# A transformer block on one Trainium2 core: the mixer's output gate copied out of PSUM by VectorE instead of ScalarE, and the three kinds of weight tile in one ring of twelve buffers

## The chip, the cores and the metric

The kernel runs on one of the eight cores of one Trainium2 chip. A time is the device time of one execution in microseconds (us), and a kernel's time is the median of its runs. The names of the engines are those of the profile: PE (TensorE, matrix multiplication; PEld is its weight load), DVE (VectorE), ACT (ScalarE), POOL (GpSimd) and SP (SyncE, which here does nothing but issue DMA transfers).

## The reference

One residual block over 512 tokens of width 1024, all in fp32. In short:

```python
mod = silu(c) @ w_ada + b_ada                        # nine rows of 1024: shift, scale, gate for three parts
sh1, s1, g1, sh2, s2, g2, sh3, s3, g3 = split(mod, 9)
x = x + 0.5 * g1 * swiglu(rms(x) * (1 + s1) + sh1, ffn1_w_in, ffn1_w_out)    # 2816 hidden features
x = x + g2 * mixer(rms(x) * (1 + s2) + sh2)
x = x + 0.5 * g3 * swiglu(rms(x) * (1 + s3) + sh3, ffn2_w_in, ffn2_w_out)

def mixer(h):
    gq, gk, gv, gz, ga, gb, cq, ckv, kr = split(h @ w_in)
    o_a = gated_delta_rule(silu(conv(gq, gk, gv)), ga, gb)       # 4 heads, chunks of 64
    o_a = rms(o_a) * silu(gz)                                    # gz is the output gate: z in the kernel
    o_b = block_causal_attention(cq, ckv, kr)                    # 4 heads, low-rank q and kv, rotary key
    return concat(o_a, rms(o_b)) @ w_out
```

## The kernel before, in words

Activations lie transposed, features on the 128 partitions and the 512 tokens along the free dimension. A product with a weight matrix goes by units of 128 output features. A unit's weights come as a raw fp32 tile of 128x8x128, which is 4 KB per partition and 512 KB in all, and are split into a high part and a low part. `wr` names the raw tile (`load`, L118, a DMA issued on SP's queue), `wh` the high part (`split_w`, L193, a cast on ACT) and `wl` the low part, raw minus high (L198, a subtraction on DVE). A few units, marked `dma`, form the low part otherwise: ACT writes minus raw, or rather its rounded copy (L195), and a DMA issued by POOL adds the raw tile onto it (L196). These are five units of the mixer's `w_in` and the first four of `ffn2_w_in`. PE then runs three matmuls for each of the eight slices of 128 inputs: high times high (L266), high weight times low activation (L267) and low weight times high activation (L268), 24 matmuls of 128x512 for a unit. The accumulator is one of the three PSUM buffers of pool `psa` (names `pa`). Five others (`psb`, names `pb`) serve all the rest.

The tiles `wr`, `wh` and `wl` come out of the pool `wp` (L85). It gives each tag its own ring of buffers, four each, twelve in all, 48 KB per partition. A raw tile is free again as soon as its split has read it, and a high or low tile only once PE has finished with the unit.

The order of the instructions in each engine's queue isn't written out by hand. A scheduler takes the instructions by the priorities that the program sets (`in_order`, `behind`), by the data that they need and by the buffers that the pools have free in its own reckoning of time, and writes one fixed queue for each engine. An engine works its queue strictly from front to back, and an instruction waits at the front until what it needs has come. So a pool of another shape moves instructions also in places that don't use it.

The program runs these stages, and the times are those of the profile. To 66 us: setup and `phase0`, which holds the first three pairs of units of the first feed-forward. 66 to 270 us: the rest of the first feed-forward's input (`ffn1`, L618, pairs of units 3 to 21), with `ada_rest` as side work. For that, SP loads the modulation weights into tiles `ar` (512 KB, pool `early`, three buffers), DVE multiplies and adds each into a sum `aa` (L549, then L551; six buffers), and PE adds up the columns of four sums at a time (L570), which frees them. 270 to 390 us: its output product (`down`). 390 to 720 us: the mixer. The last four units of `w_in` give the output gate z; `z_done` (L1919) copies each accumulator out of PSUM (L1921), and `gated_out` (L1681) reads z much later. Around them PE has the attention's scores (L1847, L1850), transposes of probabilities (L1867), and the blocks of the triangular inverse (L1553 to L1598). On ACT stand the exponentials `pr` (L168) with their ACT_TABLE_LOAD, and `mh` (L1905), on DVE the row maxima `mx` (L1856) and `ml` (L1906). 720 to 1076 us: the second feed-forward.

Of the kernel before, what the change touches and what calls it, by code (L numbers as in the profile page):

```python
# [11 lines left out]
F32 = mybir.dt.float32  # L12
F32R = mybir.dt.float32r
# [5 lines left out]
P = 128  # L19
# [22 lines left out]
class Side:  # L42


    def __init__(self, wide=1):
        self.todo, self.open, self.wide, self.at = [], [], wide, 0

    def add(self, *gens):
        self.todo.extend(gens)
# [30 lines left out]
class Block:  # L80
    def __init__(self, ctx, tc, ins, out):
        self.ctx, self.tc, self.nc, self.ins, self.out = ctx, tc, tc.nc, ins, out
        self.cp = ctx.enter_context(tc.tile_pool(name="cp", bufs=1))
        self.sp = ctx.enter_context(tc.tile_pool(name="sp", bufs=4))
        self.wp = ctx.enter_context(tc.tile_pool(name="wp", bufs=4))  # L85
        self.slots = ctx.enter_context(tc.tile_pool(name="slots", bufs=56))
        self.late = None
        self.psa = ctx.enter_context(tc.tile_pool(name="psa", bufs=3, space=bass.MemoryType.PSUM))
        self.psb = ctx.enter_context(tc.tile_pool(name="psb", bufs=5, space=bass.MemoryType.PSUM))
        self.n = 0  # L90
        self.mod = {}
        self.specs, self.ready = [], []
        self.tabled = None
# [104 lines left out]
        self.nc.vector.tensor_tensor(out=lo, in0=raw, in1=hi.bitcast(F32), op=ALU.subtract)  # L198

    def w_tiles(self):  # L200
        t = lambda dt, tag: self.wp.tile([P, 8, P], dt, tag=tag, name=self.name(tag))
        return t(F32, "wr"), t(F32R, "wh"), t(F32R, "wl")

    def unit(self, src, kts=8, dma=False):
# [536 lines left out]
    def pair_tasks(self, f, base, add):  # L741


        nc, v, w = self.nc, self.nc.vector, self.ins["ffn2_w_in"][0]
        r = {}
        flat = lambda t: t.rearrange("p k f -> p (k f)")
        A, B = slice(0, NT), slice(NT, 2 * NT)

        def tiles(names, tags, dt, bufs):
            for n, tag in zip(names, tags):  # L750
                r[n] = self.ws.tile([P, 2 * NT], dt, tag=tag, name=self.name(tag), bufs=bufs)

        def load():
            for n, c in (("g", f * P), ("u", DFF + f * P)):
                t = self.wp.tile([P, 8, P], F32, tag="wr", name=self.name("wr"))
                self.load(t, w[:, c:c + P].rearrange("(k p) f -> p k f", p=P))
                r[n] = flat(t)

        def sums():
            tiles(("x", "y"), ("sx", "sy"), F32, 1)  # L760
            v.tensor_tensor(out=r["y"][:, A], in0=r["g"][:, A], in1=r["g"][:, B], op=ALU.add)  # L761
            v.tensor_tensor(out=r["x"][:, A], in0=r["u"][:, A], in1=r["g"][:, A], op=ALU.add)

        def sums2():
            v.scalar_tensor_tensor(out=r["x"][:, B], in0=r["y"][:, A], scalar=-1.0, in1=r["u"][:, A], op0=ALU.mult,
                                   op1=ALU.subtract)
            v.tensor_tensor(out=r["y"][:, B], in0=r["u"][:, B], in1=r["x"][:, B], op=ALU.subtract)

        def hi(name, src, part=slice(0, 2 * NT)):
            def go():  # L770
                if name == "g1":
                    r["g1h"], r["g1l"] = self.slot(F32R, "gh"), self.slot(F32R, "gl")
                elif name == "y":
                    tiles(("yh", "yl"), ("yh", "yl"), F32R, 2)
                else:
                    for e in "hl":
                        r[name + e] = flat(self.wp.tile([P, 8, P], F32R, tag="w" + e, name=self.name("w" + e)))
                nc.scalar.copy(r[name + "h"], r[src][:, part])
            return go

        def lo(name, src, part=slice(0, 2 * NT)):
            def go():
                v.tensor_tensor(out=r[name + "l"], in0=r[src][:, part], in1=r[name + "h"].bitcast(F32), op=ALU.subtract)  # L783
            return go

        def early_copy(name, part):
            def go():
                if name not in r:
                    r[name] = self.slot(s=name)
                nc.scalar.copy(r[name][:, part], r["A"][:, :HALF])  # L790
            return go

        L, H = slice(0, HALF), slice(HALF, NT)

        def both():
            v.tensor_tensor(out=r["cc"], in0=r["cc"], in1=r["BC"], op=ALU.add)

        def gate0():
            v.tensor_tensor(out=r["uc"][:, H], in0=r["uc"][:, L], in1=r["BC"][:, H], op=ALU.add)
            nc.scalar.activation(r["uc"][:, H], r["uc"][:, H], AF.Silu, scale=-1.0)  # L800

        def gate1():
            nc.scalar.activation(r["cc"][:, H], r["cc"][:, H], AF.Silu, scale=-1.0)

        def act1():
            v.tensor_tensor(out=r["cc"][:, H], in0=r["cc"][:, H], in1=r["A"][:, :HALF], op=ALU.mult)

        def act0():
            v.tensor_tensor(out=r["cc"][:, L], in0=r["cc"][:, L], in1=r["uc"][:, H], op=ALU.mult)
            r["ah"] = self.slot(F32R, "ah")  # L810
            nc.scalar.copy(r["ah"], r["cc"])  # L811

        def act_low():
            al = self.slot(F32R, "al")
            v.tensor_tensor(out=al, in0=r["cc"], in1=r["ah"].bitcast(F32), op=ALU.subtract)
            self.act.append((r["ah"], al))

        r["do"] = dict(load=load, sums=sums, sums2=sums2)
        for n, src, part in (("u", "u", slice(0, 2 * NT)), ("x", "x", slice(0, 2 * NT)), ("y", "y", slice(0, 2 * NT)), ("g1", "g", B)):
            r["do"][n] = hi(n, src, part), lo(n, src, part)  # L820
        for i, (at, go) in enumerate(((-11, load), (-7, sums), (-5, sums2), (-6, hi("u", "u")), (-4, lo("u", "u")), (-4, hi("x", "x")),
                       (-3, lo("x", "x")), (-3, hi("y", "y")), (-2, lo("y", "y")), (-1, hi("g1", "g", B)),
                       (0, lo("g1", "g", B)), (1, early_copy("cc", L)), (4, early_copy("uc", L)), (7, early_copy("cc", H)),
                       (8, both), (9, gate1), (11, act1), (13, gate0), (15, act0), (16, act_low))):
            by_hand = 11 if base == 0 else 1 if base == 7 else 0
            if i >= by_hand:
                add(base + at, go)
        return r
# [21 lines left out]
    def ffn2_rest(self, ps):  # L850

        nc = self.nc
# [66 lines left out]
        w1 = self.ins["ffn2_w_in"][0]  # L919

        def raw(i):
            t = self.wp.tile([P, 8, P], F32, tag="wr", name=self.name("wr"))
            c = (i % 2) * DFF + (i // 2) * P
            self.load(t, w1[:, c:c + P].rearrange("(k p) f -> p k f", p=P))
            return t
# [1 line left out]
        raws, split, accs = {}, {3: self.next_unit(ahead=0)}, {0: ps[0], 1: ps[1], 2: ps[2]}  # L927

        def unit_split(i):
            hi, lo = (self.wp.tile([P, 8, P], F32R, tag=t, name=self.name(t)) for t in ("wh", "wl"))  # L930
            nc.scalar.copy(hi, raws[i])
            split[i] = hi, lo
            yield
            nc.vector.tensor_tensor(out=lo, in0=raws[i], in1=hi.bitcast(F32), op=ALU.subtract)
# [26 lines left out]
        for i in (4, 5, 6, 7):  # L961
            raws[i] = raw(i)
        steps = [T(0), T(1), T(2), unit_split(4), glu(0), (products, 3), T(3), unit_split(5), (do["load"],), (products, 4), T(4),
                 glu(1), unit_split(6), T(5), (products, 5), of(do["sums"]), of(do["sums2"]), unit_split(7), (d0[0],), T(6),
                 of(do["u"]), glu(2), (products, 6), of(do["x"]), (do1["load"],), T(7), of(do["y"]), of(tuple(d0[1:])),
                 (products, 7), glu(3), of(do["g1"])]
# [11 lines left out]
        k0, m = 16, 6  # L978
        units, ends = {}, {}

        def unit_load(t):
            raw = self.wp.tile([P, 8, P], F32, tag="wr", name=self.name("wr"))[:, :m, :]
            self.load(raw, w2[k0 * P:(k0 + m) * P, t * P:(t + 1) * P].rearrange("(k p) f -> p k f", p=P))
            units[t] = [raw]

        def unit_hi(t):
            units[t] += [self.wp.tile([P, 8, P], F32R, tag=w, name=self.name(w))[:, :m, :] for w in ("wh", "wl")]
            nc.scalar.copy(units[t][1], units[t][0])

        def unit_lo(t):  # L990
# [25 lines left out]
        for t in range(4, KT):  # L1016
            unit_load(t)
# [23 lines left out]
        t = KT - 1  # L1041
# [867 lines left out]
    def mixer(self, nb):  # L1909
        nc, tc = self.nc, self.tc  # L1910
# [7 lines left out]

        def z_done(i, p):  # L1919
            z = self.slot(s="z")  # L1920
            nc.scalar.copy(z, p)  # L1921
            self.zT.append(z)

        def conv_done(ct0, dst):
# [181 lines left out]
```

## Time and profile before

| | before |
|---|---|
| runs | 1077.47, 1080.53 and 1081.85 us, median 1080.53 us |
| the profiled execution | 1077.71 us, of which the span from the first to the last instruction is 1076.0 us |
| granted clock of PE, mean over the span | 0.987 |
| PE busy | 1046.7 us (97% of the span) |
| DVE, ACT, POOL busy | 689.4, 445.3 and 51.3 us |
| moved by DMA | 136.85 MB, mean 127 GB/s |

So 1.7 us of the profiled execution lie outside the span, and it was 2.8 us quicker than the median of the runs. In the lines of the profile, L12 is line 12 of the kernel, `out<-in` names tiles without their numbers, and a bracket such as [4.29 <-ACT z L1921] says that the engine had been idle 4.29 us, most of it until that instruction was done. A row of a timeline begins with start and duration in us. A row of windows gives a stretch, its length, the busy time of PE, PEld, DVE, ACT and POOL with their counts, then the clock granted to PE, the busy share of the DMA engines and the GB/s that they moved.

### The profile page before, as it was taken

Reading aid. Unit: us, or ns where it says so; the run is one execution under the profiler, and the core shown is the slowest. Engines: PE = TensorE matmul, PEld = TensorE weight load, DVE = VectorE, ACT = ScalarE, POOL = GpSimd, SP = SyncE. Lnnn points to the kernel's source line nnn. Section 1 sums busy time; section 2 is a strip of 40 time slices with the busy share of each in tenths; the row PEclk is TensorE's granted clock in tenths of the full one; section 3 lists DMA queues with packets and bytes.
Section 4 is the critical chain, followed back from the end, with each engine's and each line's share of the span. In section 5 each row is a group of like instructions: output and inputs, shape, how many; then the busy total and the mean of one; then the engine's idle time right before and its main releaser. Section 6 shows DMA issues by size and latency. Waiting matters only on the chain. (4 is left out here: it accounts for less than half of the span.)

```text
span 1076.0 us, 15659 instructions
## 1 busy us (share of the span) xinstructions
PE 1046.7 (97%) x6183; PEld 899.1 (84%) x6183; DVE 689.4 (64%) x1231; ACT 445.3 (41%) x761; POOL 51.3 (5%) x103
## 2 busy tenths in 40 slices
PE   6999999999999999998999899999999999999998
PEld 5788878788887898887778578988899999999997
DVE  4488983433577445558868644769768787777633
ACT  3342222222222245566575363465534444444322
POOL 1000000000000011102000030220000000000000
PEclk8999999999999999999999898999999999999999
DMA  9989963233698349411203001153432333233222
GB/s 274 277 240 310 301 203 99 81 98 93 199 289 263 95 120 240 113 49 40 79 25 92 26 21 39 40 126 91 129 107 79 118 115 98 83 118 99 67 71 79
DMA packets 203687, 136.85 MB, mean 127 GB/s; under 512 B 13777, under 2 KB 186590, under 8 KB 203614
## 3 DMA queue, kind: packets, MB, share of 16 engines
q1 hardware_dynamic: 202318, 131.14, 41.1%
q0 software_dynamic: 1296, 4.72, 2.4%
q8 instruction: 48, 0.79, 0.3%
q14 instruction: 25, 0.20, 0.1%
HBM read 128.63 MB, written 2.49 MB: 122 GB/s over the span
## 5 line engine op out<-in xcount | busy, mean ns | idle before, releaser
L266 PE MATMUL pa<-hh,wh 128*128 128x512 f32 (+1 forms) x597 | 227.0, 380 | 4.3 <-ACT z L1921 4.3
L268 PE MATMUL pa<-hh,wl 128*128 128x512 f32 (+1 forms) x597 | 225.0, 377 | 2.7 <-DMA wl<-wr 2.7
L267 PE MATMUL pa<-hl,wh 128*128 128x512 f32 (+1 forms) x597 | 224.8, 377 | 0.0
L193 ACT CAST wh<-wr 128x1024 fp32r<-128x1024 f32 (+1 forms) x106 | 108.0, 1019 | 258.3 <-PE pa L267 184.4
L198 DVE TENSOR_TENSOR wl<-wr,wh 128x1024 fp32r<-128x1024 f32 (+1 forms) x97 | 114.4, 1180 | 99.0 <-ACT wh L193 94.5
L266 PE MATMUL pa<-ah,wh 128*128 128x512 f32 (+1 forms) x396 | 145.5, 367 | 0.6 <-DVE xT L873 0.4
L267 PE MATMUL pa<-al,wh 128*128 128x512 f32 (+1 forms) x396 | 144.5, 365 | 0.0
L268 PE MATMUL pa<-ah,wl 128*128 128x512 f32 (+1 forms) x396 | 143.5, 362 | 0.0
L266 PEld LDWEIGHTS pa<-hh,wh 128*128 128x128 f32 x597 | 113.6, 190 | 27.2 <-ACT z L1921 4.7
L268 PEld LDWEIGHTS pa<-hh,wl 128*128 128x128 f32 x597 | 113.5, 190 | 23.1 <-DMA wl<-wr 3.3
L267 PEld LDWEIGHTS pa<-hl,wh 128*128 128x128 f32 x597 | 113.5, 190 | 19.2 <-DVE hl L453 0.4
L268 PEld LDWEIGHTS pa<-ah,wl 128*128 128x128 f32 x396 | 74.8, 189 | 12.0
L266 PEld LDWEIGHTS pa<-ah,wh 128*128 128x128 f32 x396 | 75.2, 190 | 10.4 <-ACT wh L193 1.7
L267 PEld LDWEIGHTS pa<-al,wh 128*128 128x128 f32 x396 | 75.2, 190 | 7.2
L551 DVE SCALAR_TENSOR_TENSOR aa<-ar,sc,aa 128x512 f32<-128x512 f32 x98 | 73.2, 751 | 9.7 <-DMA ar<-in_w_ada 8.5
L846 PE MATMUL pb<-fh,wh 128*128 128x256 f32 x144 | 40.7, 282 | 0.0
L848 PE MATMUL pb<-fh,wl 128*128 128x256 f32 x144 | 40.7, 283 | 0.0
L848 PE MATMUL pb<-hh,wl 128*128 128x256 f32 x144 | 40.7, 283 | 0.0
L847 PE MATMUL pb<-fl,wh 128*128 128x256 f32 x144 | 40.7, 282 | 0.0
L847 PE MATMUL pb<-hl,wh 128*128 128x256 f32 x144 | 40.7, 282 | 0.0
L846 PE MATMUL pb<-hh,wh 128*128 128x256 f32 x144 | 40.6, 282 | 0.0
L873 DVE SCALAR_TENSOR_TENSOR xT<-pa,mod,xT 128x512 f32<-128x512 f32 (+1 forms) x40 | 29.4, 736 | 17.5 <-PE pa L268 17.5
(433 smaller groups left out, 1995.0 us busy)
## 6 DMA issues: line engine op xcount, KB each, us to landing
wr<-in_ffn_w_in SPq DMA_DIRECT2D x82, 512.0 KB, 4.1
ar<-in_w_ada SPq DMA_DIRECT2D x48, 512.0 KB, 5.9
wr<-in_ffn_w_out SPq DMA_DIRECT2D x34, 512.0 KB, 3.4
ar<-in_w_ada SPq DMA_DIRECT2D x48, 256.0 KB, 4.8
wr<-in_w_in SPq DMA_DIRECT2D x21, 512.0 KB, 3.9
wr<-in_ffn_w_out SPq DMA_DIRECT2D x17, 384.0 KB, 3.4
wl<-wr POOLq DMA_DIRECT2D x9, 512.0 KB, 5.6
wr<-in_w_out SPq DMA_DIRECT2D x8, 512.0 KB, 4.8
```

Source lines behind the costliest of these rows:

```text
L193: self.nc.scalar.copy(hi, raw)
L198: self.nc.vector.tensor_tensor(out=lo, in0=raw, in1=hi.bitcast(F32), op=ALU.subtract)
L266: mm(out, wh, xh, start=start, stop=False)
L267: mm(out, wh, xl, start=False, stop=False)
L268: mm(out, wl, xh, start=False, stop=stop)
L551: nc.vector.scalar_tensor_tensor(out=acc, in0=a, scalar=sc, in1=acc, op0=ALU.mult, op1=ALU.add)
L846: mm(out, wh, xh, start=start and k == 0, stop=False, **kw)
L847: mm(out, wh, xl, start=False, stop=False, **kw)
L848: mm(out, wl, xh, start=False, stop=stop and k == 3, **kw)
L873: nc.vector.scalar_tensor_tensor(out=self.xT[t][:, ts], in0=p[:, ts], scalar=gate[:, t:t + 1], in1=self.xT[t][:, ts], op0=ALU.mult, op1=AL ...
```

## The change

It has two parts. The pool `wp` gets twelve buffers, and every tile of it takes the one tag "w", so raw, high and low tiles share one ring of the same twelve buffers. And z is copied out of PSUM by DVE.

```diff
@@ class Block, __init__
-        self.wp = ctx.enter_context(tc.tile_pool(name="wp", bufs=4))
+        self.wp = ctx.enter_context(tc.tile_pool(name="wp", bufs=12))
@@ w_tiles
-        t = lambda dt, tag: self.wp.tile([P, 8, P], dt, tag=tag, name=self.name(tag))
+        t = lambda dt, tag: self.wp.tile([P, 8, P], dt, tag="w", name=self.name(tag))
         return t(F32, "wr"), t(F32R, "wh"), t(F32R, "wl")
...
@@ the same at L755, L777, L922, L930, L982 and L987, for instance
-                t = self.wp.tile([P, 8, P], F32, tag="wr", name=self.name("wr"))
+                t = self.wp.tile([P, 8, P], F32, tag="w", name=self.name("wr"))
...
@@ mixer, z_done
             z = self.slot(s="z")
-            nc.scalar.copy(z, p)
+            nc.vector.tensor_copy(z, p)
             self.zT.append(z)
```

Each engine still has the instructions that it had, but for z, and the queues stand in another order. Three places follow, each with the queue of before and then that of the change. The numbers tell tiles of one name apart.

First, SP's queue in the first feed-forward. This is the stretch of before that runs from the load ar_802 on; `ar` are modulation weights, `wr` raw weights of feed-forward units, whose order of use is wr_627, 633, 669, 731, 766, 820, 855, 942, 977, 1034, 1070.

```order
L118 DMA ar_802<-in_w_ada 128x2x512
L118 DMA ar_851<-in_w_ada 128x2x512
L118 DMA ar_886<-in_w_ada 128x2x512
L118 DMA wr_977<-in_ffn_w_in 128x8x128
L118 DMA ar_891<-in_w_ada 128x2x512
L118 DMA ar_973<-in_w_ada 128x2x512
L118 DMA ar_1008<-in_w_ada 128x2x512
L118 DMA wr_1034<-in_ffn_w_in 128x8x128
L118 DMA ar_1012<-in_w_ada 128x2x512
L118 DMA wr_1070<-in_ffn_w_in 128x8x128
```

And this is the stretch of the changed queue with the same modulation loads.

```order
L118 DMA wr_731<-in_ffn_w_in 128x8x128
L118 DMA ar_851<-in_w_ada 128x2x512
L118 DMA ar_886<-in_w_ada 128x2x512
L118 DMA wr_766<-in_ffn_w_in 128x8x128
L118 DMA ar_891<-in_w_ada 128x2x512
L118 DMA ar_973<-in_w_ada 128x2x512
L118 DMA wr_820<-in_ffn_w_in 128x8x128
L118 DMA ar_1008<-in_w_ada 128x2x512
L118 DMA ar_1012<-in_w_ada 128x2x512
L118 DMA wr_855<-in_ffn_w_in 128x8x128
```

Beside ar_1012 the queue of before has come to wr_1070 and the changed one to wr_855, four units less. In the same stage L570 of the sum aa_664, the first of its four, moves on PE from behind the unit of wr_1164 to the third matmul of the unit of wr_731, and two small transposes (L1079, L1086) move there with it.

Second, ACT and DVE where the first copy of z stands, z_5224. This is ACT before; `wh_5738` is the high part of a unit of `w_out`.

```order
L193 CAST wh_5738<-wr_5737 128x1024
L168 ACT_TABLE_LOAD
L168 ACTIVATE pr_5213,al_5053<-pb_5204,mx_5211 128x256
L168 ACTIVATE pr_5218,al_5056<-pb_5205,mx_5216 128x256
L1905 ACTIVATE mh_5220<-pb_5182,cwT_808 128x512
L1921 COPY z_5224<-pa_5129 128x512
```

In the changed queue of ACT another cast stands ahead of the same table load, and z is gone. The cast wh_5738 waited for PE; wh_5883 waits for its load and for DVE.

```order
L193 CAST wh_5883<-wr_5882 128x1024
L168 ACT_TABLE_LOAD
L168 ACTIVATE pr_5213,al_5053<-pb_5204,mx_5211 128x256
L168 ACTIVATE pr_5218,al_5056<-pb_5205,mx_5216 128x256
L1905 ACTIVATE mh_5220<-pb_5182,cwT_808 128x512
L193 CAST wh_6004<-wr_6003 128x1024
```

In the changed queue of DVE the copy stands here:

```order
L1206 TENSOR_TENSOR Y_5202<-pb_5197,mk_2377 128x512
L1854 MEMSET pb_5204 64x64
L1856 TENSOR_REDUCE mx_5211<-pb_5204 128x1
L1854 MEMSET pb_5205 64x64
L1856 TENSOR_REDUCE mx_5216<-pb_5205 128x1
L1906 SCALAR_TENSOR_TENSOR ml_5221<-pb_5182,cwT_808,mh_5220 128x512
L1921 COPY z_5224<-pa_5129 128x512
L1206 TENSOR_TENSOR t_5239<-t_5138,mk_2377 128x512
```

So z is copied right behind ml_5221, which reads mh_5220 of ACT. On PE the two matmuls that stood last ahead of the unit that waits for this copy now stand ahead of the scores.

Third, ACT at the end of the mixer, where the first units of `ffn2_w_in` are split. Before:

```order
L193 CAST wh_6368<-wr_6367 128x1024
L475 ACTIVATE sq_6354<-xT_106 128x256
L195 ACTIVATE wl_6369<-wr_6367 128x1024
L475 ACTIVATE sq_6388<-xT_106 128x256
L443 COPY rb_6393<-pb_6391 128x256
L193 CAST wh_6419<-wr_6418 128x1024
L461 ACTIVATE hh_6301<-tm_6317,mod_2754 128x256
L195 ACTIVATE wl_6420<-wr_6418 128x1024
```

In the changed queue the rows from the copy rb_6393 to hh_6301 look like this:

```order
L195 ACTIVATE wl_6420<-wr_6418 128x1024
L475 ACTIVATE sq_6354<-xT_106 128x256
L475 ACTIVATE sq_6388<-xT_106 128x256
L443 COPY rb_6393<-pb_6391 128x256
L193 CAST wh_6466<-wr_6465 128x1024
L461 ACTIVATE hh_6301<-tm_6317,mod_2754 128x256
```

The low part wl_6420 of the second unit has moved up by four rows of the norm's work, and what stood ahead of it has gone further up: wl_6369 stands ahead of the next to last block of `mh` casts, and wh_6419 behind that block, in front of sq_6156 and hn_6179 (L1711). The cast wh_6419 now also waits for the DMA that adds wr_6367 onto wl_6369, because it takes over that raw tile's buffer.

Two smaller moves are not shown. On PE the transposes of qro (L1768) come ahead of four dense matmuls that they followed. And at the mixer's start the raw loads wr_3539, wr_3619 and wr_3703 of `w_in` move on SP's queue from ahead of the ten loads `ur` of `mla_w_uq` and `mla_w_ukv` to behind them.

More of the change, by code (lines that the diff above doesn't have):

```diff
@@ L776, in go @@
                     for e in "hl":
[L777 removed]
+                        r[name + e] = flat(self.wp.tile([P, 8, P], F32R, tag="w", name=self.name("w" + e)))
                 nc.scalar.copy(r[name + "h"], r[src][:, part])
@@ L921, in raw @@
         def raw(i):
-            t = self.wp.tile([P, 8, P], F32, tag="wr", name=self.name("wr"))
+            t = self.wp.tile([P, 8, P], F32, tag="w", name=self.name("wr"))
             c = (i % 2) * DFF + (i // 2) * P
@@ L929, in unit_split @@
         def unit_split(i):
-            hi, lo = (self.wp.tile([P, 8, P], F32R, tag=t, name=self.name(t)) for t in ("wh", "wl"))
+            hi, lo = (self.wp.tile([P, 8, P], F32R, tag="w", name=self.name(t)) for t in ("wh", "wl"))
             nc.scalar.copy(hi, raws[i])
@@ L981, in unit_load @@
         def unit_load(t):
-            raw = self.wp.tile([P, 8, P], F32, tag="wr", name=self.name("wr"))[:, :m, :]
+            raw = self.wp.tile([P, 8, P], F32, tag="w", name=self.name("wr"))[:, :m, :]
             self.load(raw, w2[k0 * P:(k0 + m) * P, t * P:(t + 1) * P].rearrange("(k p) f -> p k f", p=P))
@@ L986, in unit_hi @@
         def unit_hi(t):
-            units[t] += [self.wp.tile([P, 8, P], F32R, tag=w, name=self.name(w))[:, :m, :] for w in ("wh", "wl")]
+            units[t] += [self.wp.tile([P, 8, P], F32R, tag="w", name=self.name(w))[:, :m, :] for w in ("wh", "wl")]
             nc.scalar.copy(units[t][1], units[t][0])
```

## The prediction

> **What bounds the kernel now.** The page's busy times come first: PE works through nearly the whole span, so the time is PE's work, plus its idle time, plus what it loses at a lower clock.
>
> ```profile
> PE 1046.7 (97%) x6183; PEld 899.1 (84%) x6183; DVE 689.4 (64%) x1231; ACT 445.3 (41%) x761; POOL 51.3 (5%) x103
> ```
>
> That leaves 1076.0 - 1046.7 = 29.3 us of idle PE. PE's own list of waits (us in total, times, longest) names the places that the change can reach.
>
> ```profile
> PE pa L266 <- ACT z L1921: 4.3, 1, 4.3
> PE pb L1768 <- DVE qro L1834: 2.8, 2, 2.6
> PE pa L268 <- DMA wl<-wr: 2.7, 2, 2.0
> ```
>
> The largest is the copy that the change moves, and the third is the low part of a weight tile. No raw weight load is in that list. The windows around the first and the third wait show a second loss: the clock that PE is granted, the third number from the end.
>
> ```profile
> 596.00:600.00 4.00, 0.32 (x2) 0.00 (x0) 2.06 (x4) 3.85 (x8) 0.00 (x0) 0.83 0.09 13
> 600.00:604.00 4.00, 3.39 (x13) 2.98 (x14) 2.43 (x4) 0.56 (x2) 0.00 (x0) 0.50 0.34 119
> 604.00:608.00 4.00, 4.00 (x22) 3.33 (x21) 2.32 (x4) 0.85 (x2) 0.00 (x0) 0.82 0.02 4
> 718.00:720.00 2.00, 1.99 (x9) 1.99 (x10) 1.72 (x5) 1.47 (x4) 0.84 (x1) 0.53 1.19 292
> 720.00:722.00 2.00, 2.00 (x14) 2.00 (x13) 0.63 (x2) 0.51 (x1) 0.00 (x0) 0.62 0.97 219
> ```
>
> Behind each wait PE runs at about half its clock for a while. Behind z that loses 3.39 x 0.50 + 4.00 x 0.18 = 2.4 us, and behind the low tile 1.99 x 0.47 + 2.00 x 0.38 = 1.7 us. So a removed wait can be worth more than its own length, and a new one can cost more.
>
> **The copy of z.** ACT's timeline shows why PE waited for it: the copy is a short one at the end of a queue.
>
> ```profile
> 596.12 1.05 ACT L193 CAST wh<-wr 128x1024 fp32r<-128x1024 f32 x1 [6.80 <-PE pa L267]
> 597.19 1.28 ACT L168 ACT_TABLE_LOAD   x1
> 598.48 0.47 ACT L168 ACTIVATE pr<-pb,mx 128x256 f32<-128x256 f32 x1
> ...
> 599.40 0.69 ACT L1905 ACTIVATE mh<-pb,cwT 128x512 fp32r<-128x512 f32 x1
> 599.97 0.59 ACT L1921 COPY z<-pa 128x512 f32<-128x512 f32 x1
> 600.61 0.80 PE L266 MATMUL pa<-hh,wh 128*128 128x512 f32 x1 [4.29 <-ACT z L1921]
> ```
>
> ACT stood 6.80 us at a cast whose buffer PE still read, and the table load, the exponentials and mh came behind it. In the changed queue that cast is another, which has no wait for PE, so the table load falls into the idle time and the exponentials are held by their maxima alone. DVE's timeline gives these, and ml; the groups give the price of a copy out of PSUM on DVE.
>
> ```profile
> 596.45 0.42 DVE L1856 TENSOR_REDUCE mx<-pb 128x1 f32<-128x256 f32 x1
> ...
> 600.12 0.75 DVE L1906 SCALAR_TENSOR_TENSOR ml<-pb,cwT,mh 128x512 fp32r<-128x512 f32 x1 [1.69 <-ACT mh L1905]
> L316 DVE COPY xT<-pb 128x512 f32<-128x512 f32 x8 | 5.3, 688 | 4.1 <-PE pb L315 4.1
> ```
>
> The first exponential starts with the first maximum, at about 596.3, and mh follows 0.92 us behind it as before (598.48 to 599.40), at 597.3. It ends 0.69 later at 598.0, ml takes 0.75 to 598.7, and the copy 0.69 to 599.4, where ACT's copy was done at 600.6. The scores now stand behind two more matmuls of 0.23 us, so all of it comes 0.4 later: 599.8. PE, which has done the same work by then, goes on 0.8 us earlier. The bounds are 1.3 us of gain, if those two matmuls don't delay the scores, and 0.4 of loss, if the cast in front turns out to hold the table load after all and the copy only changes engines with ml ahead of it. I take 0.8. A wait of about 3.5 us stays, and I leave the 2.4 us of slow clock behind it as they are: the shorter wait of 2.0 us at 718 brought one too. The Trainium skill, page "TensorE: Matmul & The Clock Gate", section "Part 1: The HAM clock gate", states that PE falls to half clock only after at least one idle window of about 3.4 us. By that rule the wait of 2.0 us would have cost no clock, which the rows at 718 to 722 contradict. The other three copies of z cost DVE 3 x 0.69 us and spare ACT 3 x 0.59 us; nothing of PE waited for them, and DVE is busy 64%, so they are put at nothing. If DVE were late there, PE would pay at most the 0.1 us by which each copy is longer.
>
> **The low tile at 718.** POOL's, ACT's and PE's timelines show its making.
>
> ```profile
> 710.98 1.05 ACT L195 ACTIVATE wl<-wr 128x1024 fp32r<-128x1024 f32 x1
> 712.32 0.85 POOL L196 DMA_DIRECT2D wl<-wr  x1 [3.26 <-ACT wl L195]
> 718.01 0.51 PE L268 MATMUL pa<-hh,wl 128*128 128x256 f32 x1 [1.96 <-DMA wl<-wr]
> ```
>
> The tile is wl_6420. In the changed order L195 stands four rows of the norm higher, some 4 us earlier, so its DMA lands at about 714, ahead of 716. That saves 2.0 us and the 1.7 us of clock. The third unit's tile is next; it moves up too, and I see no wait for it. The bounds are 3.7 and 0 us, if that next tile is as late; I take 3.7, because both moved.
>
> The price is paid on ACT higher up, where the cast wh_6419 waits for the first of these DMAs, with sq and hn queued behind it. DVE, POOL and PE wait for hn in turn.
>
> ```profile
> 694.24 0.62 ACT L1711 ACTIVATE hn<-o 128x512 f32<-128x512 f32 x1
> wl<-wr POOLq DMA_DIRECT2D x9, 512.0 KB, 5.6
> ```
>
> With 5.6 us to landing, and L195 issued ahead of the last mh casts, I put hn 1 to 2 us later. Most of that is slack; I take 0.5 us, bounds 0 and 2.
>
> **qro.** PE's transposes of qro now stand four dense matmuls further ahead, so PE waits 4 x 0.23 = 0.9 us longer there and has that work to do afterwards. Bounds 0 and 0.9; I take 0.9.
>
> **The weight loads of the first feed-forward.** Here nothing waits today, and the ring takes the lead away. The groups give the split's two steps, the DMA part the landing times, SP's timeline the issues.
>
> ```profile
> L193 ACT CAST wh<-wr 128x1024 fp32r<-128x1024 f32 (+1 forms) x106 | 108.0, 1019 | 258.3 <-PE pa L267 184.4
> L198 DVE TENSOR_TENSOR wl<-wr,wh 128x1024 fp32r<-128x1024 f32 (+1 forms) x97 | 114.4, 1180 | 99.0 <-ACT wh L193 94.5
> wr<-in_ffn_w_in SPq DMA_DIRECT2D x82, 512.0 KB, 4.1
> ar<-in_w_ada SPq DMA_DIRECT2D x48, 512.0 KB, 5.9
> 57.62 1.41 SPq L118 DMA_DIRECT2D ar<-in_w_ada  x3
> ...
> 148.43 3.70 SPq L118 DMA_DIRECT2D ar<-in_w_ada  x3
> 60.00:100.00 40.00, 40.00 (x177) 32.44 (x176) 35.13 (x50) 15.90 (x21) 0.00 (x0) 1.00 0.94 289
> 66.25 0.39 PE L266 MATMUL pa<-hh,wh 128*128 128x512 f32 x1
> 66.48 0.39 PE L267 MATMUL pa<-hl,wh 128*128 128x512 f32 x1
> ```
>
> PE begins unit 0 of this stretch at 66.25 and needs a new one every 24 x 0.23 = 5.5 us. Before, SP ran the weights some four units ahead; changed, each stands behind two or three ar loads. Counted in the changed queue from the ar load at 57.62 on, wr_731 (unit 3) is the 10th load, wr_1034 (unit 9) the 28th, wr_1164 (unit 12) the 39th, wr_1355 (unit 16) the 49th. The lower bound lets the DMA run without a gap: the first lands at 57.62 + 5.9 = 63.5, each next one 524 KB / 289 GB/s = 1.81 us later, and cast and subtraction add 2.2. Unit 3 is then ready at 82.0 and needed at 82.75; unit 9 at 114.6 and 115.75; unit 12 at 134.5 and 132.25, 2.2 us late; unit 16 at 152.6 and 154.25. So PE loses 2.2 us, in pieces too small to cost clock, or nothing if the DMA goes a tenth faster. The upper bound lets every ar go out only when it did before, since each waits for DVE to free one of three buffers: wr_1261 (unit 14) then follows the ar at 148.43 and is ready at 148.4 + 4.1 + 2.2 = 154.7, where PE needs it at 143.25 plus the column sums, 144.3: 10.4 us late. Which it is nearer to is told by what held those ar loads.
>
> ```profile
> 137.90 1.06 PE L570 MATMUL pb<-aa,ones 128*32 128x512 f32 x8
> 140.85 0.48 DVE L549 TENSOR_SCALAR aa<-ar,sc 128x512 f32<-128x512 f32 x1
> ```
>
> The seventh sum had to wait for PE's L570 at 137.90 to free one of six buffers, and with it the ar loads. The changed order frees that buffer in unit 3, and DVE no longer subtracts weight tiles far ahead. The two transposes that move into unit 3 wait for loads that SP issues ahead of wr_731, so wr_731 is later than they. So I go near the lower bound: 2.0 us.
>
> **Other stages.** At the mixer's start three weight loads now follow the ten loads ur. Those ten no longer stand behind a wait for a weight buffer and go out earlier, so I put this at nothing. Part of the 2.7 us of waits for wl<-wr, 0.7, lies there and bounds the gain; if the lead is gone, one tile's DMA of 5.6 us bounds the loss. In the output product and in the second feed-forward the loads shift as well, but PE waits for no load there today, and between two of them lie 5.5 us of a unit's matmuls: nothing, with one landing of 4.1 us as the loss if that cover is gone.
>
> **Sum.** -0.8 (z) - 3.7 (low tile) + 0.5 (hn) + 0.9 (qro) + 2.0 (loads) = -1.1 us. The profiled execution would go from 1077.7 to 1076.6, and the median of the runs, 2.8 us above it, from 1080.5 to 1079.4.
>
> **The rivals.** The first ends slower: the ar loads stay as they were, and the weights behind them starve PE between units 3 and 14. For it speaks that DVE is busy 35.1 of 40 us there and that SP's queue can't pass a waiting ar; against it the freed buffer. From about 5 us of lateness on it outweighs the gains. At its full 10.4 in place of 2.0 the time is 1079.4 + 8.4 = 1087.8, and a piece above 2 us adds its 1.7 us of clock. The second is faster: a wait shorter than a full window of idle time costs no clock, so that z's 2.4 us go as well, and the DMA runs fast enough that the loads cost nothing: 1079.4 - 2.4 - 2.0 = 1075.0, or 1074.1 without the 0.9 for qro. This is what the clock rule of the Trainium skill would make of the z wait. The row at 718 speaks against it, the remaining 3.5 us being so near a window for it. The third is that it does nothing: low tile and z find another wait close behind, the loads are hidden, and 1080.5 stays.
>
> **How the numbers follow.** A measurement of this kernel can tell about 0.5%, 5.4 us, from no change. My forecast has a chance of 0.48, of which 0.05 falls below 1075.1 and 0.01 above 1085.9. The starved loads have 0.22, the faster rival 0.22 and the third 0.08. So faster 0.27, same 0.50, slower 0.23. The range goes from a little below the faster rival, 1073, to a little above the starved one, 1089.
>
> **What would show it.** Right: the wait for z about 3.5 us and named after DVE; no wait for wl<-wr at 716 and a clock of 1.00 in 718 to 722; a few waits of L266 or L268 between 82 and 150 us, 2 us together. The loads are wrong if that sum is above 5 or nothing, and the clock argument if the wait for z stays and no half clock follows. The forecast is wrong if PE's idle time in the first feed-forward alone exceeds 6 us, or if a wait appears in a stage that I left out, the second feed-forward above all.

## The result and the profile after

The changed kernel takes 1091.72 us in the median (1090.99 to 1093.93, five runs), and the kernel before 1080.53 us (1076.56 to 1081.85, five runs). The ratio is 1.0118, with a 95% interval of 1.0092 to 1.0145: slower by 1.2%, where no measurable change was forecast. The profiled execution took 1093.93 us with a span of 1091.9 us. That is 16.2 us more than the profiled one of before, but that one lay 2.8 us below its median and this one 2.2 us above, which leaves the 11.2 us between the medians.

The page's busy times of the changed kernel show no more work than before:

```profile
PE 1051.4 (96%) x6183; PEld 901.6 (83%) x6183; DVE 693.4 (64%) x1235; ACT 441.6 (40%) x757; POOL 53.0 (5%) x103
```

The count of matmuls is the same, and PE's idle time went from 29.3 to 40.5 us. PE's list of waits of the changed kernel says at which instructions:

```profile
PE pa L268 <- DMA wl<-wr: 7.2, 2, 4.2
PE pa L266 <- ACT hh L461: 4.0, 1, 4.0
PE pa L266 <- DVE z L1921: 3.8, 1, 3.8
...
PE pb L1768 <- DVE qro L1834: 2.7, 1, 2.7
...
PE pa L268 <- DVE wl L198: 1.6, 3, 1.2
```

The wait for z went from 4.3 to 3.8. The one for DMA-made low tiles went from 2.7 to 7.2, and one for `hh` is new. To place these, here are four stretches of before, with the length, PE's busy time first, and the granted clock third from the end:

```profile
66.00:160.00 94.00, 94.00 (x419) 76.33 (x418) 83.15 (x153) 29.37 (x38) 0.00 (x0) 1.00 0.87 267
390.00:435.00 45.00, 43.01 (x312) 40.36 (x311) 26.42 (x55) 27.83 (x46) 7.03 (x9) 1.00 0.88 212
...
640.00:690.00 50.00, 49.45 (x354) 43.55 (x352) 27.62 (x57) 19.07 (x44) 6.49 (x7) 0.90 0.11 32
690.00:745.00 55.00, 52.91 (x390) 50.70 (x389) 41.51 (x101) 31.23 (x62) 11.22 (x14) 0.97 0.41 97
```

The same of the changed kernel, with the four places in these stretches and behind z where its clock is low:

```profile
66.00:160.00 94.00, 92.20 (x402) 72.83 (x401) 80.36 (x147) 27.98 (x36) 0.00 (x0) 1.00 0.86 262
390.00:435.00 45.00, 37.76 (x277) 37.09 (x276) 18.20 (x44) 19.92 (x33) 7.04 (x9) 0.89 0.70 174
...
640.00:690.00 50.00, 49.36 (x422) 41.23 (x421) 28.52 (x53) 18.68 (x41) 11.77 (x12) 1.00 0.14 43
690.00:745.00 55.00, 48.09 (x342) 45.31 (x341) 33.45 (x88) 25.14 (x56) 12.53 (x15) 0.91 0.47 106
...
410.00:414.00 4.00, 4.00 (x23) 4.00 (x22) 0.16 (x1) 0.00 (x0) 0.31 (x1) 0.57 1.06 276
420.00:428.00 8.00, 6.04 (x30) 6.04 (x31) 4.07 (x11) 5.89 (x9) 0.85 (x1) 0.57 0.39 76
...
612.00:618.00 6.00, 5.16 (x18) 4.40 (x19) 4.10 (x7) 0.93 (x2) 0.00 (x0) 0.50 0.00 0
...
732.00:741.00 9.00, 8.18 (x35) 7.65 (x36) 5.04 (x14) 3.72 (x8) 1.72 (x2) 0.50 0.84 198
```

Idle time is length less busy time, and the time lost to the clock is busy time by what the clock lacks to 1. After against before:

- 66 to 160 us, the first feed-forward: 94.00 - 92.20 = 1.8 us of idle PE where there was none.
- 390 to 435 us, where the mixer makes its first units of `w_in` (the latents): idle 7.24 against 1.99, so +5.25, and 37.76 x 0.11 = 4.2 by the clock. Together +9.4.
- 640 to 690 us: 49.45 x 0.10 = 4.9 us of slow clock are gone.
- 690 to 745 us: idle 6.91 against 2.09, so +4.8, and by the clock 48.09 x 0.09 - 52.91 x 0.03 = +2.7. Together +7.5.
- the wait for z: 0.5 less, with the half clock behind it as before.

The sum is 1.8 + 9.4 - 4.9 + 7.5 - 0.5 = 13.3 of the 15.9 us by which the spans differ. The rest isn't placed, since the stages of the changed kernel lie up to 16 us later in the same stretches.

**The latents.** In the changed kernel SP's queue issues the first raw tiles of `w_in` at 392, not 378 us. POOL's timeline, of the changed kernel first, shows the DMAs that finish the low tiles:

```profile
401.77 1.04 POOL L196 DMA_DIRECT2D wl<-wr  x1 [8.37 <-ACT sq L475]
406.00 0.85 POOL L196 DMA_DIRECT2D wl<-wr  x1 [3.19 <-PE pa L268]
413.69 0.71 POOL L179 TENSOR_TENSOR ry<-ve,mhalf 128x2 f32<-128x2 f32 x1 [6.84 <-DVE ve L519]
414.37 0.86 POOL L196 DMA_DIRECT2D wl<-wr  x1
```

Before:

```profile
398.02 1.04 POOL L196 DMA_DIRECT2D wl<-wr  x1 [7.34 <-ACT wl L195]
401.13 0.85 POOL L196 DMA_DIRECT2D wl<-wr  x1 [2.07 <-ACT wl L195]
403.81 0.84 POOL L196 DMA_DIRECT2D wl<-wr  x1 [1.83 <-ACT wl L195]
```

The first stands 3.8 us later, the third 10.6: it is now queued behind `ry`, an inverse root of the norm, which waits for DVE. ACT's and PE's timelines of the changed kernel show that ACT had ended its part of the third tile at 408.75, and when PE got the tiles:

```profile
407.70 1.05 ACT L195 ACTIVATE wl<-wr 128x1024 fp32r<-128x1024 f32 x1
409.20 0.39 PE L268 MATMUL pa<-hh,wl 128*128 128x256 f32 x1 [3.07 <-DMA wl<-wr]
421.96 0.58 PE L268 MATMUL pa<-hh,wl 128*128 128x256 f32 x1 [4.17 <-DMA wl<-wr]
```

So two waits of 3.07 and 4.17 us, each with its stretch of clock 0.57 beside it.

**The second feed-forward's first units.** ACT's and PE's timelines of the changed kernel:

```profile
705.12 1.05 ACT L193 CAST wh<-wr 128x1024 fp32r<-128x1024 f32 x1 [3.84 <-DMA wl<-wr]
...
730.83 1.04 ACT L193 CAST wh<-wr 128x1024 fp32r<-128x1024 f32 x1 [5.55 <-DMA wr<-in_ffn_w_in]
...
732.34 0.58 PE L266 MATMUL pa<-hh,wh 128*128 128x256 f32 x1 [4.04 <-ACT hh L461]
```

At 705 the cast waits for an accumulating DMA that still reads the raw tile whose buffer it takes. On ACT `hn` stands behind that cast, DVE waits 3.45 us for hn, and the next update of `xT` stands behind that on DVE, for which PE waits. DVE's and PE's timelines:

```profile
707.04 0.69 DVE L1712 TENSOR_REDUCE gs<-hn 128x4 f32<-128x512 f32 x1 [3.45 <-ACT hn L1711]
708.65 0.38 PE L266 MATMUL pa<-mh,wh 128*128 128x256 f32 x1 [1.27 <-DVE xT L2065]
```

At 730 the next cast waits for its raw load. The chain of work that ended last tells why that load came late (a row has start, duration and what ran):

```profile
717.52 6.47 DMA wl<-wr
...
724.05 6.70 DMA wr<-in_ffn_w_in
...
730.83 1.04 ACT wh L193
```

The load waits in SP's queue until the DMA issued at 717.52 has landed, at 723.99; it goes out at 724.05 and lands at 730.75. The activation `hh` stands behind the cast on ACT, and PE stands 4.04 us for it.

### The profile page after: what moved, and what is told of

It reads as the page before. It is cut to its first block, busy times and chain, and to the rows that moved or that the text cites. A ratio compares the mean times of both kernels' runs of the same rounds, so it can differ in the third digit from the quotient of the medians.

```text
span 1091.9 us, 15612 instructions
## 1 busy us (share of the span) xinstructions
PE 1051.4 (96%) x6183; PEld 901.6 (83%) x6183; DVE 693.4 (64%) x1235; ACT 441.6 (40%) x757; POOL 53.0 (5%) x103
## 4 chain that ended last, share of the span: by engine, by line
PE 75%; DVE 8%; DMA 8%; ACT 4%; issue 3%; SPq 1%; POOL 1%; ACTq 0%; DVEq 0%; POOLq 0%
PE pa L266 16%; PE pa L268 16%; PE pa L267 16%; DMA wr<-in_ffn_w_in 5%; PE pb L846 5%; PE pb L847 5%; PE pb L848 5%; DMA wl<-wr 2%; DVE wl L198 1%; DVE aa L551 1%; ACT wh L193 1%; PE pb L414 1%; PE pb L1847 1%; DMA ar<-in_w_ada 1%; PE pb L266 1%
## 5 line engine op out<-in xcount | busy, mean ns | idle before, releaser
L266 PE MATMUL pa<-hh,wh 128*128 128x512 f32 (+1 forms) x597 | 230.7, 386 | 8.0 <-ACT hh L461 4.0
L268 PE MATMUL pa<-hh,wl 128*128 128x512 f32 (+1 forms) x597 | 228.0, 382 | 9.0 <-DMA wl<-wr 7.2
L198 DVE TENSOR_TENSOR wl<-wr,wh 128x1024 fp32r<-128x1024 f32 (+1 forms) x97 | 114.5, 1182 | 101.0 <-PE pa L267 52.8
L268 PE MATMUL pa<-ah,wl 128*128 128x512 f32 (+1 forms) x396 | 143.5, 362 | 0.0
L266 PEld LDWEIGHTS pa<-hh,wh 128*128 128x128 f32 x597 | 116.1, 194 | 31.6 <-ACT hh L461 4.2
L268 PEld LDWEIGHTS pa<-hh,wl 128*128 128x128 f32 x597 | 115.9, 194 | 31.8 <-DMA wl<-wr 7.7
L267 PEld LDWEIGHTS pa<-hl,wh 128*128 128x128 f32 x597 | 116.0, 194 | 18.6 <-DVE hl L453 0.4
L268 PEld LDWEIGHTS pa<-ah,wl 128*128 128x128 f32 x396 | 74.8, 189 | 12.0
L266 PEld LDWEIGHTS pa<-ah,wh 128*128 128x128 f32 x396 | 75.2, 190 | 10.4 <-issue 2.5
```

Of the source, the lines that this page charges most:

```text
L266: mm(out, wh, xh, start=start, stop=False)
L267: mm(out, wh, xl, start=False, stop=False)
L268: mm(out, wl, xh, start=False, stop=stop)
```

## The experiments

Theory A: the shared ring costs the time. Theory B: the copy of z on VectorE costs it. All runs are timed against the kernel before on the same chip. A time is the median; a ratio comes from all runs, so that it isn't quite the quotient of two medians, and carries its 95% interval.

**Each half alone.** The ring without the copy (of the changed kernel):

```diff
-            nc.vector.tensor_copy(z, p)
+            nc.scalar.copy(z, p)
```

> The ring alone: z is copied by ScalarE as before. Theory A, that the shared ring costs the time, because raw loads and casts now wait for buffers that matmuls and accumulating DMAs hold: 1088 to 1094 us, with the two long waits for wl<-wr near 409 and 422 us and the wait for hh near 732 us of the changed kernel in place. Theory B, that the copy of z on VectorE costs it, by the order that it brings among the scores: 1078 to 1083 us, and none of these waits.

Measured: 1095.05 us, ratio 1.0150 (1.0125 to 1.0175), 1 us above what A expected. Its long waits of PE are nearly those of the changed kernel:

```profile
PE pa L268 <- DMA wl<-wr: 7.1, 3, 3.2
PE pa L266 <- ACT hh L461: 4.1, 1, 4.1
PE pa L266 <- ACT z L1921: 3.9, 1, 3.9
```

The copy without the ring is the opposite edit, made in the kernel before.

> The copy of z on VectorE alone, with the three rings of four. Theory A: 1076 to 1083 us, no wait for wl<-wr longer than the 2.0 us of before, and the wait for z at most 4.3 us. Theory B: 1088 us or more, with new waits between 570 and 640 us.

Measured: 1081.05 us, ratio 1.0020 (1.0004 to 1.0035). The time is as A expected, but the wait for z grew, where it was to stay at 4.3 or less:

```profile
PE pa L266 <- DVE z L1921: 5.2, 1, 5.2
PE pa L268 <- DMA wl<-wr: 2.8, 2, 1.9
```

A holds and B falls: the ring alone loses all of it and more, the copy alone next to nothing. The two depend on each other, though. The wait for z gets longer by the copy alone (4.3 to 5.2) and shorter by the ring alone (4.3 to 3.9). And the slow clock between 640 and 690 us, which the changed kernel has lost, is still there with the ring alone (0.90 in that stretch).

**Raw tiles in a ring of their own.** The changed kernel, with four buffers for raw tiles and eight that high and low tiles share.

```diff
-        t = lambda dt, tag: self.wp.tile([P, 8, P], dt, tag="w", name=self.name(tag))
+        t = lambda dt, tag: self.wp.tile([P, 8, P], dt, tag=tag if tag == "wr" else "w",
+                                         name=self.name(tag), bufs=4 if tag == "wr" else 8)
...
```

> Raw tiles have their own ring of four again, high and low tiles share one of eight, z stays on VectorE. Theory A, in the form that it is the raw tiles' lost buffers: the raw loads run ahead again, the first feed-forward has no wait, and the time is 1076 to 1084 us. If sharing between high and low tiles is what costs, or the copy of z, it stays at 1088 us or more.

Measured: 1081.78 us, ratio 1.0023 (1.0009 to 1.0038), the same as the copy alone. PE's idle time in the first feed-forward is nothing again, the waits for `wl<-wr` are 2.7 us, and that for `hh` is gone. So what costs time is that raw tiles compete with split tiles for buffers; that high and low tiles share theirs does not.

**POOL's queue.** The changed kernel, with the small inverse roots `ry` of up to two columns taken from POOL to DVE, so that the third DMA of the latents has nothing to stand behind. The edit moves the roots of the later norm as well, so it acts at both places.

```diff
-        if n <= 8:
+        if 2 < n <= 8:
             nc.gpsimd.tensor_tensor(out=y, in0=v, in1=self.mhalf[:, :n], op=ALU.pow)
```

> The changed kernel, but the two-column reciprocal roots ry of the norms are formed on VectorE by the Newton steps that the kernel has for wider ones, so that GpSimd's queue holds no ry ahead of an accumulating DMA there. If the wait of 4.2 us at 422 us comes from that place in GpSimd's queue (the third DMA issued at 414.4, right behind ry at 413.7, though ScalarE's part was done at 408.8): that wait goes, with its clock of 0.50 to 0.66 after it, 5 to 8 us together, so 1084 to 1087 us. If the late raw loads alone hold it, the wait stays above 3 us and the time at 1090 to 1094 us.

Measured: 1084.86 us, ratio 1.0059 (1.0036 to 1.0081), half of the loss. POOL issues the third DMA at 409.11 in place of 414.37, the waits for `wl<-wr` fall to 4.9 us, and that for `hh` isn't in the list any more. A wait of 3.3 for `dg` L433, part of the norm whose root is now on DVE, is new. The same edit in the kernel before is the control:

> The kernel before with the two-column roots ry on VectorE, the reference for the ring with that edit, which took 1084.9. In the kernel before three accumulating DMAs stood ahead of ry on GpSimd's queue, so nothing is unblocked: 1077 to 1083 us if the gain of 7 us was that blocking. If the edit is simply a shorter path through the norm, it gains 4 us or more here too: 1076 us or less.

Measured: 1080.36 us, ratio 1.0023 (1.0009 to 1.0037). The edit itself gains nothing; it only pays where the ring has used up the lead.

**No low tile made by DMA.** The changed kernel with all nine of these low tiles subtracted on DVE like the others.

```diff
     def split_w(self, raw, hi, lo, dma=False):
         self.nc.scalar.copy(hi, raw)
-        if dma:
+        if False:
```

> The changed kernel, but no low tile is made by a DMA: the nine units that had ScalarE write minus raw and a DMA add it have VectorE subtract, as all others. Theory A1, that the ring's loss sits at those nine units, where the accumulating DMA holds a raw buffer some 8 us longer and a late one delays a cast or a raw load in a queue: within 3 us of the same edit of the kernel before, and no wait above 2 us at either norm but for VectorE. Theory A2, that raw loads come too late everywhere: still 8 us or more slower than that.

Measured: 1072.43 us (1070.68 to 1075.58), ratio 0.9955 (0.9940 to 0.9971): faster than the kernel before, by 0.45%. The stretches in which the changed kernel lost, here:

```profile
66.00:160.00 94.00, 91.28 (x398) 72.18 (x397) 80.69 (x146) 28.06 (x36) 0.00 (x0) 1.00 0.86 259
390.00:435.00 45.00, 45.00 (x334) 43.02 (x334) 32.15 (x63) 23.67 (x42) 4.87 (x5) 1.00 0.54 151
...
640.00:690.00 50.00, 49.52 (x386) 44.53 (x386) 31.95 (x67) 20.43 (x48) 6.00 (x7) 1.00 0.14 43
690.00:745.00 55.00, 52.46 (x370) 48.91 (x369) 46.12 (x102) 26.41 (x51) 7.97 (x9) 1.00 0.31 87
```

PE is busy for all of 390 to 435 at full clock. Yet SP issues the same three raw tiles as late as in the changed kernel, in this one first:

```profile
392.10 8.74 SPq L118 DMA_DIRECT2D wr<-in_w_in  x3
```

and in the changed kernel:

```profile
392.39 8.74 SPq L118 DMA_DIRECT2D wr<-in_w_in  x3
```

So these late loads alone cost nothing. They cost time when the low tile also has to go through ACT, POOL's queue and a DMA. From POOL's issue at 401.77 to PE's start on the tile at 409.20 this took 7.4 us for the first one, where a subtraction on DVE takes 1.2 (the group of L198), and ACT's part takes another 1.0 ahead of the issue. The edit takes away two things at once, the long making of the low tile and the DMA's long hold on the raw tile's buffer. The waits at 409 and 422 show the first and the chain from 717.52 the second, but no run has one without the other. The control is the same edit in the kernel before:

> The kernel before with the same edit, as the reference for the run ahead of it: VectorE has nine subtractions of 1.2 us more near the two norms. 1078 to 1085 us; under both theories alike.

Measured: 1081.43 us, ratio 1.0021 (1.0002 to 1.0040). With the lead of the kernel before, the way of making the tile costs 0.2%. Against this control the ring with the copy takes 0.9955 / 1.0021 = 0.993 of the time.

**Which of the nine.** The changed kernel with the five `w_in` tiles alone made by DVE:

```diff
         for c in (2056, 2184, 2312, 2440, 2568):
-            cols(w, c, True)
+            cols(w, c)
```

> The changed kernel, but the five w_in weight tiles that GpSimd's accumulating DMA had made (the latents' stage, from 400 us on) get their low half from VectorE; the four ffn2 ones keep the DMA. Theory A1 (two separate losses, each at the place where DMA-made low tiles stand in the shared ring): the loss between 390 and 435 us goes, 5.2 us of idle TensorE and some 4.2 us of half clock, so 1.0118 falls by about 9.4 of 1079 us to 1.003, 1.001 to 1.005; the wait of hh L461 near 730 us stays at 3 to 5 us. Theory A2 (one loss: the raw loads late at 400 us shift the whole ring, and the wait at 730 us is its echo): both go, 0.994 to 0.997.

Measured: 1079.94 us, ratio 1.0012 (0.9992 to 1.0031). And with the four `ffn2_w_in` tiles alone:

```diff
-        up(ins["ffn2_w_in"][0], 0, 2, True)
+        up(ins["ffn2_w_in"][0], 0, 2)
```

> The changed kernel, but the four ffn2 weight tiles that the accumulating DMA had made (700 to 735 us) get their low half from VectorE; the five w_in ones keep the DMA. A1: the waits of the casts at 705 and 731 us and of hh L461 go, 4.8 us of idle TensorE and some 2.7 us of half clock between 690 and 745 us, so 1.0118 falls by about 7.5 us to 1.005, 1.003 to 1.007; the two wl<-wr waits of 7.2 us between 400 and 425 us stay. A2: nothing goes that does not go at 400 us: 1.010 to 1.012.

Measured: 1085.75 us, ratio 1.0075 (1.0056 to 1.0093). Of PE's long waits at the two places there is left, with the five by DVE:

```profile
PE pa L266 <- ACT hh L461: 3.7, 1, 3.7
```

and with the four by DVE:

```profile
PE pa L268 <- DMA wl<-wr: 7.3, 2, 4.1
```

Each edit removes one loss and leaves the other, so theory A1 holds, two separate losses, and A2 falls. From 1.0118 the first takes 1.06%, the second 0.43%, together 1.49%, and both at once 1.63%. Each of these ratios is uncertain by about 0.2%, so the sum and the edit at both places agree. The second took less than the 0.7% expected, and its ratio lies just outside the range.

**The first copy of z.** In the kernel before, the cast wh_5738 is ordered behind the copy, which stays on ScalarE.

```diff
-        self.nc.scalar.copy(hi, raw)
+        ins = self.nc.scalar.copy(hi, raw).ins
+        if self.z0 and self.n > self.zn + 100:
+            self.follow(ins, self.z0)
+            self.z0 = None
...
-            nc.scalar.copy(z, p)
+            ins = nc.scalar.copy(z, p).ins
+            if i == 0:
+                self.z0, self.zn = ins.name, self.n
```

> The kernel before, z on ScalarE, but the cast that made ScalarE wait 6.80 us for matmuls is ordered behind the first copy of z. If that cast and not the engine of the copy is what PE's wait of 4.3 us hangs on: the exponentials start with their maxima at about 596.3, z is out near 598.5 and PE goes on 2 us earlier, with up to 2.4 us of clock: 1076 to 1078.5 us. If the copy's engine matters, the wait stays at 4 us or more and the time at 1079 to 1082 us.

Measured: 1075.67 us, ratio 0.9988 (0.9973 to 1.0002), which is not told from no change. The wait for z fell from 4.3 to 3.5 us, by 0.8 where 2 had been expected. So the cast in front did hold the copy, but with the cast out of the way ACT waits for the first maximum ahead of the table load, whose 1.28 us stay in the path (L1859 of this kernel is L1856 of before):

```profile
595.64 1.28 ACT L168 ACT_TABLE_LOAD   x1 [7.06 <-DVE mx L1859]
```

In the changed kernel the table load runs ahead of the maximum, as the prediction had it, and the exponential starts with its maximum:

```profile
605.85 1.28 ACT L168 ACT_TABLE_LOAD   x1
609.69 0.47 ACT L168 ACTIVATE pr<-pb,mx 128x256 f32<-128x256 f32 x1 [2.56 <-DVE mx L1856]
```

The ring without DMA-made low tiles and with z on ScalarE:

> The ring without any DMA-made low tile, with z copied by ScalarE as before. If the copy on VectorE is worth what the ring alone lost beside the changed kernel (1.0150 against 1.0118), this is 0.3% above the ring without the DMA on VectorE: 0.9985, 0.997 to 1.000. If the engine of the copy does not matter (theory B0), 0.9955, 0.994 to 0.997.

Measured: 1078.65 us, ratio 1.0005 (0.9985 to 1.0024), beside 0.9955 with z on VectorE. And this order of the casts in it:

> As the one before, with the weight casts on ScalarE ordered behind the first z copy. If what the first z copy waits for is the cast ahead of it, the wait at z falls from about 4 to 3.5 us or under and the time by 0.1 to 0.3% against the ring with z on ScalarE; otherwise the same time within 0.1%. The earlier run of this order on the kernel before gave 0.9988.

Measured: 1083.05 us, ratio 1.0051 (1.0034 to 1.0068). Both miss what was expected: the engine of the copy is worth 0.5% here, more than the 0.3%, and the order loses 0.5% where it should have gained a little, though its wait for z did fall to 3.5. One window places it. With z on ScalarE:

```profile
640.00:690.00 50.00, 49.55 (x349) 42.77 (x348) 26.84 (x54) 17.69 (x42) 6.61 (x7) 0.90 0.11 32
```

With the casts behind z:

```profile
640.00:690.00 50.00, 48.05 (x353) 41.36 (x353) 24.50 (x46) 16.13 (x36) 10.98 (x11) 0.80 0.11 33
```

Against 1.00 with z on VectorE, the clock alone loses 49.55 x 0.10 = 5.0 and 48.05 x 0.20 = 9.6 us. The first is about what the ratios differ by, 0.5% or 5.4 us. These are single executions, and the clock differs from run to run. But the mean clock over all runs of each stands in the same order: 0.994 with z on VectorE, 0.988 with z on ScalarE, 0.984 with the casts behind z. The slow stretch lies some 40 us behind the copy of z, where PE works on the triangular inverse. Shortly ahead of it PE waits for `on` at the transposes of L1900. With z on ScalarE:

```profile
PE pb L1900 <- DVE on L1206: 1.4, 2, 1.0
```

In the ring without DMA-made low tiles and z on VectorE:

```profile
PE pb L1900 <- DVE on L1206: 0.6, 1, 0.6
```

The slow stretch is there in every profile in which the waits at this place come to 0.9 us or more: the kernel before and its variants, the ring with raw tiles apart, and the ring with z on ScalarE in all three versions. It is missing in the five that have one wait of 0.6 us: the changed kernel and the ring with z on VectorE in its other versions. Each version has one profile. Why that wait is shorter there, and whether it causes the slow clock, wasn't tried and stays open.

No version beat the ring without DMA-made low tiles and with z on VectorE: 1072.43 us, 0.9955 of the kernel before.

## Why the prediction was wrong, point by point

- **Other stages: the step that failed.** The prediction wrote for the mixer's start "so I put this at nothing", with one tile's DMA of 5.6 us as the loss, and for the second feed-forward "nothing, with one landing of 4.1 us as the loss if that cover is gone". The first place lost 9.4 us and the second 7.5. The reason given was that the ten loads `ur` go out earlier. They do, but what matters there is when the raw tiles in front of them go out, 14 us later than before, and that the tiles from them are made by DMA. The prediction had the prices, a late low tile at 718 and a cast that waits until an accumulating DMA gives a buffer back, but it put them on the first two tiles of `ffn2_w_in` alone. At the mixer's start the first low tile took 7.4 us from the issue on where a subtraction takes 1.2, so the lead of the raw loads had been its cover. In the second feed-forward the DMA issued at 717.52 kept the next raw load back until 724. Taking the DMA away in either place removes that place's loss. The sign that the prediction named last, a wait in the second feed-forward, came true.
- **The bound was too low as well.** It held one landing. It left out POOL's queue, where `ry` put the third DMA back to 414.37 although ACT was done at 408.75, and the half clock behind each wait. The latter was the prediction's own rule, applied at 718 and not here.
- **The low tile at 718, -3.7: right at the place, wrong in the sum.** There is no wait for `wl<-wr` between 716 and 722, and the clock is full in 718 to 728 (PE busy 9.83 of 10). "The third unit's tile is next; it moves up too, and I see no wait for it" failed: the next raw load was late, and the wait came at 732 as one for `hh`, 4.04 us with half clock from 732 to 741. The bound of 0 was too kind. The 7.5 us of this stretch are what is left after the gain at 718.
- **The loads of the first feed-forward, +2.0: right.** 1.8 us, in waits at L268, and no clock lost. The rival of starved loads, 10.4 us, did not come about. In the eight profiles in which all three kinds of tile share the ring this idle time was between 0.8 and 3.8 us, though the traces of all eight show the same order of operations in this stage. So that 1.8 came so near to 2.0 is in part luck: it is a matter of how the transfers happen to run, at the edge of being late.
- **z, -0.8: nearly right, for the reason given.** The wait went from 4.3 to 3.8, near the predicted "about 3.5", named after DVE, and half clock followed again: 5.16 x 0.50 = 2.6 us, predicted 2.4. The gain comes from the cast that the ring moves away, not from the engine: the copy alone, in the kernel before, lengthens the wait by 0.9 us, which is more than the bound of 0.4 us of loss.
- **hn, +0.5: right in kind, somewhat larger.** The cast did wait for the DMA, 3.84 us at 705, and hn stood behind it. No wait of PE is named after hn, but the wait of 1.27 us for `xT` at 708.65 hangs on it, and the kernel before has no such wait. That is within the bounds of 0 and 2, and it is part of the 7.5 us above.
- **qro, +0.9: wrong, and small.** The wait is 2.7, as before.
- **What was left out on the good side:** the slow clock between 640 and 690 us of before, 4.9 us, was not in the rows that the prediction read, so that it could not be counted as something to gain. Without this gain the change would by estimate have cost some 16 us in the median in place of 11.2. The ring alone, whose profile still has the slow stretch, did cost 1.5%, about 16 us.
- **The rivals.** Slower was given 0.23, by a mechanism at the wrong place: raw loads that starve the first feed-forward. The range ended at 1089, 2.7 us short. The faster rival, that a wait below a full window costs no clock, falls at the wait of 3.07 us at 409, behind which the clock was 0.57 from 410 to 414. The waits of 3.83, 4.04 and 4.17 us had half clock behind them too, but they are no shorter than the 3.5 us at which the prediction saw a full window near, so they can't tell.

## What to carry to other kernels

When a pool of one ring replaces rings for each kind of tile, look for the tiles whose making takes longest, here a low tile that goes through ACT, POOL's queue and a DMA, and ask at each of them how much lead its input had and how long its making holds the buffer that it reads. Here a late load cost nothing where 1.2 us of work followed, and several microseconds where a queue and a DMA followed. And cost a wait together with the clock that PE loses behind it: in this kernel that was most of the wait's length again.

## What the runs showed of the hardware

- **The clock can fall while PE is busy.** The windows of the kernel before, up to the slow stretch:

```profile
606.00:629.00 23.00, 22.98 (x165) 17.33 (x163) 12.25 (x25) 11.77 (x30) 1.01 (x1) 1.00 0.01 2
629.00:642.00 13.00, 12.06 (x144) 8.66 (x143) 7.64 (x15) 5.98 (x13) 7.45 (x7) 1.00 0.13 42
...
642.00:654.00 12.00, 12.00 (x82) 10.24 (x83) 4.68 (x8) 2.92 (x7) 0.00 (x0) 0.57 0.03 7
```

  From 642 to 654 us PE has no idle time by the profile, which models the ends of matmuls, and a clock of 0.57, and in the 36 us ahead it was idle for 0.96 us in all, most of it in two waits. The Trainium skill, page "TensorE: Matmul & The Clock Gate", section "Part 1: The HAM clock gate", puts half clock, in its table of the two states, behind at least one idle window of about 3.4 us; this trace shows a fall with far less. What the matmuls there have to do with it, many of them of 32x32 and 64x64, stays open.
- **The runs of one kernel differ by their clock.** In 85 runs of the kernel before beside the experiments, times go from 1073.3 to 1083.1 us, and the mean clock from 0.992 down to 0.981. A straight line through them gives 0.77 us for each 0.001 of clock and leaves 17% of the variance. So most of what looks like scatter between runs goes with how much slow clock a run gets.
- **The DMAs that add a tile onto a tile landed later in the changed kernel.** The median of the nine, from issue to landing, was 5.6 us in the profile of before and 6.5 in that of the changed kernel:

```profile
wl<-wr POOLq DMA_DIRECT2D x9, 512.0 KB, 6.5
```

  The first of them, with DMA engines busy 85% from 400 to 410 us, took 7.4 from issue to PE's start.
